# Hybrid attention and convolution block: the first two seven-product column pairs in turns, their operand sets spread over more products, and a spare weight buffer in the place of the convolution's tiles

## The chip, the cores and the metric

One core of one Trainium2 chip runs the whole kernel. The metric is the device time of one execution in microseconds (us); lower is better. A result is the median of several runs.

## The reference

One layer of a residual block over 2048 tokens of 1024 features, in float32:

```python
h    = rmsnorm(x, norm_g)
proj = einsum('bsd,de->bse', h, w_in)         # 1024 -> 6144 columns
q, k, v, z_att, gb, gc, u, z_conv, g_att, g_conv = split(proj)
att    = chunked_rel_attention(q, k, v, rel_bias)   # 8 heads, own chunk of 64 and 8 to the left
y_att  = (att * silu(z_att)) @ w_att_out
vconv  = causal_depthwise_conv(gc * u, conv_w, conv_b)   # width 3
y_conv = (gb * vconv * silu(z_conv)) @ w_conv_out
m   = sigmoid(g_att) * y_att + sigmoid(g_conv) * y_conv
out = rmsnorm(x + m @ w_out, final_norm_g)
```

Eight of the ten column groups of `w_in` have 512 columns, the two gates (`g_att`, `g_conv`) 1024 each.

## The kernel before

**Numbers.** Every matmul is made of three passes (`passes`, L132 to L137): each operand is split into a high part and a remainder, and high x high, high x low and low x high are added up. A split (`split_into` L122 and L123, `split_pair` L128 and L129, `raw_split` L344 and L345) is a cast on ScalarE and a subtraction on VectorE.

**Stages.** The projection runs over two halves of 1024 tokens, each over 24 pairs of column tiles (2 x 128 columns). A half of tokens is two blocks of 512 (c = 0, 1), the 1024 features are two halves (k = 0, 1), and a pair is two column tiles (n = 0, 1): a 2 x 2 x 2 block product. It is done with seven products in place of eight (`ORDER = (1, 2, 6, 5, 7, 4, 3)`), each 12 matmuls of 128 x 512. Its left operands are combinations of the pair's four weight blocks (`operand`, L375 to L399), its right operands combinations of the four token blocks b11, b12, b21, b22 (`operand_steps`, L348 to L363: product 1 uses b11, 2 uses b21, 6 uses b11 + b12, and so on). The seven results are put together by VectorE as they come (L749 to L769), and an evacuation function takes each finished 128 x 512 tile on: gates go through tanh and to memory from ScalarE's DMA queue (`ev_gate`), the convolution's pairs go through `conv_pair`, queries, keys and values to memory. The attention runs later, beside the second half's products; then come the output projections.

**The start.** The normalization needs sums over the tokens, which are not there at once. The first `PLAIN = 3` pairs of the first half are therefore done as plain products: 12 groups q = 0 to 11, in the order pair, token block c, column tile n, each of 24 matmuls on tokens that are scaled by `norm_g` alone (`raw_split`), and the result is multiplied by the token's factor when it is evacuated (`scaled`, L607, the operation whose output is named `c`). For q below 4 ScalarE copies the bank out first. Beside these groups VectorE normalizes the token blocks (L304) and makes right operands for the seven-product pairs (tiles t1.. to t7.., named by product and feature tile: t10l is the low part of product 1's first). `between(q)` lists what is made after which group: it calls for a set of right operands at each q above 5 until five are made, and the last two follow beside the first seven products. Weights of the plain pairs are split by `weights0` (tiles `w0`) at the end of groups 2, 3, 6 and 7.

**What orders the work.** The part with the plain groups stands in a manual schedule: PE, VectorE and ScalarE run its operations in the order of the program. Outside of it a scheduler orders each engine's queue, and it also moves later operations up between those of the manual part. Each engine, and each DMA queue (SP's for loads and stores, ScalarE's for gate tiles), then goes through its queue strictly in order, so that an instruction that waits holds up all behind it. PSUM has three banks for these products (`ps_d`). Raw weights have four buffers of 512 KB (`ww`: two per pair), split weights four (`wr`, tile `wc` or `w0`), token blocks four (`xs`). The split weights of product s + 2 are made while product s runs; each `wc` is also stored to memory for the second half (L399), and the store of s - 2 must have landed before the buffer takes s + 2.

**Names.** I number the seven-product work of the first half from product 0, the first after the plain groups; pairs are counted from 0 in the order in which they run. Pairs 0 to 2 are plain. Pair 3 is a gate; before the change pairs 4 and 5 are the first two of the convolution, and four gates follow one by one between the other convolution pairs up to pair 15; pairs 16 to 23 are queries, keys, values and z. The convolution's tiles come from a pool `cva` that is open from the start.

Of the kernel before, what the change touches and what calls it, by code (L numbers as in the profile page):

```python
# [8 lines left out]
F32 = mybir.dt.float32  # L9
# [8 lines left out]
P = 128  # L18
# [5 lines left out]
CH = 512  # L24
# [16 lines left out]
def block_kernel(ctx, tc, xb, xt, wp_in, wy, wo, bias, ng, fg, cw, cb, out):  # L41
# [225 lines left out]
    s_pool = fp("s", 2)  # L267
    conv_stack = ExitStack()
    cva = conv_stack.enter_context(tc.tile_pool(name="cva", bufs=2))

    blocks = {}
    ops = {}
# [97 lines left out]
    def load_raw(p, n):  # L370
        r = ww.tile([P, 2, 4, P], F32, tag="w", name="wraw")
        raws[p, n] = r
        nc.sync.dma_start(r, wp_in[p % NPAIR, n])
# [89 lines left out]
    def conv_pair(b):  # L463
# [5 lines left out]
        def conv(c, x, y):  # L469
            a = cva.tile([P, 2 + CH], F32, tag="a", name="cva")  # L470
            av[c] = a
# [36 lines left out]
    conv_gate = lambda *g: [x for b in range(4) for x in (C + 2 * b, C + 2 * b + 1, *g[b:b + 1])]  # L508
    order = [[*range(G, G + 4), *conv_gate(G + 4, G + 5, G + 6, G + 7), *range(Q, Q + 8)]]
    order.append([G + 3, G + 4, *range(G, G + PLAIN), *range(Q, Q + 8), *conv_gate(), G + 5, G + 6, G + 7])  # L510
# [49 lines left out]
    mid0, mid1 = names[PLAIN:NPAIR - 2], names[NPAIR + 2:]  # L560
    seq = [(p, i) for p in mid0 for i in ORDER]
    seq += together(*names[NPAIR - 2:NPAIR], ending)
# [18 lines left out]
    for sb, src in ((cw_sb, cw), (cb_sb, cb)):  # L581
        nc.sync.dma_start(sb, src)
    warm = ep.tile([P, CH], BF16, tag="e", name="warm")
    nc.vector.memset(warm, 0.0)
# [45 lines left out]
    def between(q):  # L630

        if q == 4 or q == 5:
            for k in range(8):
                normalize(tt_[q - 4][k], k, rb[q - 4])
        elif q == 6:
            for j in range(4):
                third(0, j)
        if q in (6, 7):
            for n in range(2):
                copied.pop(0)()  # L640
        if q > 5 and len(built) < 5:
            built.append(next(steps))
# [67 lines left out]
    for s, (p, i) in enumerate(seq):  # L710
        half = p // NPAIR
        n = names.index(p)
        if due and due[0] <= s:
            due.pop(0)
            next(turned)
        if half == 0 and i == 1 and n + 1 < NPAIR:
            for k in range(2):
# [5 lines left out]
        while nw < min(len(seq), s + ahead + 1):  # L723
            operand(*seq[nw])
            nw += 1
        if half == 0 and len(built) < 7 and s:
            built.append(next(steps))
# [58 lines left out]
        if n == NPAIR + 2 + PLAIN + 16 and i == 1:  # L786
            conv_stack.close()
            gp = pool("gp", 5)
# [178 lines left out]
```

## Time and profile before

| what | us |
|---|---|
| median of three runs | 1554.11 |
| lowest and highest of them | 1553.26, 1556.15 |
| the profiled execution, its own time | 1557.6 |
| its span, first to last instruction | 1555.8 |
| TensorE busy in the span | 1516.6 |
| VectorE, ScalarE busy | 1039.7, 680.1 |
| mean granted clock of TensorE | 0.992 |

Busy time of TensorE is the time in which any matmul is in flight; since matmuls overlap, a busy TensorE is not one at its peak, and the pace is read from the distance of their starts. The granted clock is the share of full speed that TensorE was given. A row of waits says who waited for whom, how long in total, how often, and the longest. In the rows in order of time the first number is the start in us from the start of the span, the second the duration, and the bracket gives the engine's idle time before the row and what ended it. `PEld` is the load of weights into TensorE, which overlaps the matmuls; `SPq` and `ACTq` are the queues that issue DMA.

### The profile page before, as it was taken

What the parts mean: (1) busy time and instruction counts of PE and PEld (TensorE: products, weight loads), DVE (VectorE), ACT (ScalarE), POOL (GpSimd) and SP (SyncE); (2) the same over time, 40 slices, a digit from 0 to 9 for tenths busy, and PEclk for the clock granted to TensorE, in tenths of its full rate; (3) what the DMA queues carried; (4) which work ended last, traced back from release to release, by engine and by line L of the source; (5) the groups of instructions that cost most, each with busy time, mean ns of one, the idle gap of its engine ahead of it and who ended that gap; (6) DMA issues with size and microseconds to landing.
All of it is one profiled execution on the core that took longest, in us unless ns stands there. A gap on an engine that the chain in (4) does not pass through costs nothing.

```text
span 1555.8 us, 21590 instructions
## 1 busy us (share of the span) xinstructions
PE 1516.6 (97%) x7396; PEld 1267.9 (81%) x7396; DVE 1039.7 (67%) x2078; ACT 680.1 (44%) x1250; POOL 155.0 (10%) x294
## 2 busy tenths in 40 slices
PE   9899999999998999999999999999999999999997
PEld 6678888888776788888888888888888888888886
DVE  7977789796668654666666767677755574445544
ACT  6353353443325343555666556666665231112111
POOL 0000000000000001223222222322220000000000
PEclk9999999999999999999999999999999999999999
DMA  5288999988987835999898776888889945365131
GB/s 209 77 285 307 339 353 327 364 310 305 319 301 262 279 122 177 329 339 341 294 290 272 228 265 228 262 261 272 263 278 322 304 162 200 102 233 193 62 109 68
DMA packets 159406, 389.45 MB, mean 250 GB/s; under 512 B 19904, under 2 KB 40384, under 8 KB 159296
## 3 DMA queue, kind: packets, MB, share of 16 engines
q1 hardware_dynamic: 129088, 302.06, 56.2%
q0 software_dynamic: 20992, 69.22, 13.6%
q10 hardware_dynamic: 9216, 16.78, 2.9%
q8 instruction: 59, 0.97, 0.3%
q14 instruction: 51, 0.42, 0.1%
HBM read 236.99 MB, written 150.99 MB: 249 GB/s over the span
## 4 chain that ended last, share of the span: by engine, by line
PE 83%; DVE 9%; ACT 2%; DMA 2%; issue 2%; POOL 0%; SPq 0%; ACTq 0%; DVEq 0%; POOLq 0%
PE ps_d L137 20%; PE ps_d L135 20%; PE ps_d L136 20%; PE ps_d L876 4%; PE ps_d L874 4%; PE ps_d L875 4%; PE ps_s L190 4%; PE po L228 4%; PE ps_t L210 3%; DVE ptl L216 1%; DVE ps_s L196 1%; DMA wc<-wc 1%; DVE xs L304 1%; ACT pr L200 1%; DMA vv<-v 0%
## 5 line engine op out<-in xcount | busy, mean ns | idle before, releaser
L200 ACT ACTIVATE pr<-ps_s,nmax 128x640 f32<-128x640 f32 (+4 forms) x128 | 93.4, 730 | 96.7 <-DVE nmax L196 96.1
L158 POOL DMA_DIRECT2D q<-q x128 | 66.7, 526 | 681.3 <-DVE wc L123 602.5
L196 DVE CUSTOM_DVE_ANT_0 ps_s<-ps_s,bs 128x640 f32<-128x640 f32 (+4 forms) x128 | 95.4, 745 | 53.8 <-PE ps_s L190 53.2
L122 ACT CAST wc<-wraw 128x512 fp32r<-128x512 f32 x120 | 73.6, 621 | 114.2 <-PE ps_d L137 94.2
L202 ACT ACTIVATE pr<-pr,rs 128x640 f32<-128x640 f32 (+4 forms) x128 | 97.8, 764 | 27.3 <-DVE rs L201 27.2
L190 PE MATMUL ps_s<-kk,q 128*128 128x320 f32 (+1 forms) x448 | 97.4, 333 | 2.9 <-ACT pr L200 2.8
L135 PE MATMUL ps_d<-mid,wy 128*128 128x512 f32 x256 | 99.6, 389 | 0.0
L136 PE MATMUL ps_d<-mid,wy 128*128 128x512 f32 x256 | 99.6, 389 | 0.0
L137 PE MATMUL ps_d<-mid,wy 128*128 128x512 f32 x256 | 99.6, 389 | 0.0
L216 DVE TENSOR_TENSOR ptl<-ps_t,pth 128x640 fp32r<-128x640 f32 (+4 forms) x128 | 94.3, 736 | 6.6 <-ACT pth L215 6.0
L215 ACT CAST pth<-ps_t 128x640 fp32r<-128x640 f32 (+4 forms) x128 | 80.0, 625 | 41.0 <-PE ps_t L210 40.0
L123 DVE TENSOR_TENSOR wc<-wraw,wc 128x512 fp32r<-128x512 f32 x120 | 82.2, 689 | 13.7 <-ACT wc L122 13.5
L210 PE MATMUL ps_t<-ident,pr 128*128 128x128 f32 x560 | 83.9, 276 | 1.1 <-DVE ptl L216 0.6
L883 ACT ACTIVATE sq<-y 128x512 f32<-128x512 f32 x32 | 20.2, 632 | 146.0 <-DVE y L878 141.3
L228 PE MATMUL po<-pth,vv 128*128 128x256 f32 x336 | 79.1, 271 | 1.8 <-DMA vv<-v 1.6
L228 PE MATMUL po<-ptl,vv 128*128 128x256 f32 x336 | 78.3, 281 | 0.2 <-DVE ptl L216 0.2
L874 PE MATMUL ps_d<-wo,mh 128*128 128x512 f32 x192 | 74.7, 389 | 0.0
L875 PE MATMUL ps_d<-wo,mh 128*128 128x512 f32 x192 | 74.7, 389 | 0.0
L876 PE MATMUL ps_d<-wo,ml 128*128 128x512 f32 x192 | 74.7, 389 | 0.0
L190 PEld LDWEIGHTS ps_s<-kk,q 128*128 128x128 f32 x448 | 67.0, 190 | 7.8 <-ACT pr L200 7.4
L878 DVE SCALAR_TENSOR_TENSOR y<-ps_d,y 128x512 f32<-128x512 f32 x32 | 22.1, 692 | 76.0 <-PE ps_d L876 75.9
L210 PEld LDWEIGHTS ps_t<-ident,pr 128*128 128x128 f32 x560 | 63.2, 140 | 11.4 <-DVE ptl L216 2.1
(370 smaller groups left out, 4183.8 us busy)
## 6 DMA issues: line engine op xcount, KB each, us to landing
wc<-wc SPq DMA_DIRECT2D x294, 512.0 KB, 4.8
wraw<-wp_in SPq DMA_DIRECT2D x54, 512.0 KB, 5.9
q<-q POOLq DMA_DIRECT2D x128, 128.0 KB, 4.9
gl<-gate SPq DMA_DIRECT2D x64, 256.0 KB, 3.2
mid<-mid SPq DMA_DIRECT2D x64, 256.0 KB, 5.2
bs<-bias POOLq DMA_DIRECT2D x32, 320.0 KB, 7.2
gate<-c ACTq DMA_DIRECT2D x34, 256.0 KB, 4.7
v<-vst SPq DMA_DIRECT2D x64, 128.0 KB, 4.7
```

The source lines that it names most:

```text
L135: nc.tensor.matmul(ps, lhsT=w[:, 0, k, :], rhs=rh[:, cs], start=(first and k == 0), stop=False)
L136: nc.tensor.matmul(ps, lhsT=w[:, 0, k, :], rhs=rl[:, cs], start=False, stop=False)
L137: nc.tensor.matmul(ps, lhsT=w[:, 1, k, :], rhs=rh[:, cs], start=False, stop=(last and k == len(rhs) - 1))
L190: nc.tensor.matmul(ps[:, i, :m], lhsT=q[s][:, g * P:(g + 1) * P], rhs=kk[:, k1 - n + i * m:k1 - n + (i + 1) * m], start=(s == 0), stop=(s ...
L196: nc.vector.tensor_tensor_reduce(out=view, in0=view, in1=bv, scale=-0.125, scalar=3.0e38, op0=ALU.add, op1=ALU.min, accum_out=nmax)
L200: nc.scalar.activation(out, view, AF.Exp, bias=nmax, scale=-1.0, accum_out=rs)
L210: nc.tensor.transpose(out=ps[:, j * P:(j + 1) * P], in_=pr[:, j * P:(j + 1) * P], identity=ident)
L216: nc.vector.tensor_sub(lo[:, js, qs], src, hi[:, js, qs].bitcast(F32))
L228: nc.tensor.matmul(ps[:, (g0 + a) * P:(g0 + b) * P], lhsT=vv[:, g0 + j, :], rhs=s[:, j, a * P:b * P], start=(i == 0 and s is pt[0]), stop= ...
L874: nc.tensor.matmul(ps, lhsT=mh[:, gs], rhs=wh, start=(k == 0), stop=False)
L875: nc.tensor.matmul(ps, lhsT=mh[:, gs], rhs=wl, start=False, stop=False)
L876: nc.tensor.matmul(ps, lhsT=ml[:, gs], rhs=wh, start=False, stop=(k == KT - 1))
```

## The change

Five things are edited.

- **Order of the pairs.** The first half's gates 4 and 5 now run as pairs 4 and 5, directly after pair 3, and the convolution starts with pair 6. Gates 6 and 7 stay between convolution pairs.
- **Pairs 3 and 4 in turns.** Their fourteen products run as 1, 2 of pair 3, then 1, 2 of pair 4, then 6 of both, 5 of both, 7 of both, 4 of both, 3 of both.
- **Right operands.** `between(q)` asks for one set after group 6 and one after group 7 (products 1 and 2). The other five are asked for at every odd product from product 1 on.
- **Loads.** Pair 4's raw weights are loaded in the row of early loads, and no longer at pair 3's first product. Pair 5's first half goes into a buffer of its own.
- **The spare buffer.** A pool `extra` (one buffer of 512 KB) takes the place at which the pool `cva` stood; at the first product of pair 6 it is closed and `cva` is opened there.

```diff
-    conv_stack = ExitStack()
-    cva = conv_stack.enter_context(tc.tile_pool(name="cva", bufs=2))
+    spare = ExitStack()
+    extra = spare.enter_context(tc.tile_pool(name="extra", bufs=1))
+    pools = []
...
     def load_raw(p, n):
-        r = ww.tile([P, 2, 4, P], F32, tag="w", name="wraw")
+        r = (extra if (p, n) == (names[PLAIN + 2], 0) else ww).tile([P, 2, 4, P], F32, tag="w", name="wraw")
...
-            a = cva.tile([P, 2 + CH], F32, tag="a", name="cva")
+            a = pools[0].tile([P, 2 + CH], F32, tag="a", name="cva")
...
-    order = [[*range(G, G + 4), *conv_gate(G + 4, G + 5, G + 6, G + 7), *range(Q, Q + 8)]]
+    order = [[*range(G, G + 6), *conv_gate(G + 6, G + 7), *range(Q, Q + 8)]]
...
-    seq = [(p, i) for p in mid0 for i in ORDER]
+    seq = together(*mid0[:2], [*((i, k) for k in range(2) for i in (1, 2)), *((i, k) for i in ORDER[2:] for k in range(2))])
+    seq += [(p, i) for p in mid0[2:] for i in ORDER]
...
+    for k in range(2):
+        load_raw(4, k)
...
-        if q > 5 and len(built) < 5:
+        if q in (6, 7):
             built.append(next(steps))
...
-        if half == 0 and i == 1 and n + 1 < NPAIR:
+        if n == PLAIN + 3 and i == 1:
+            spare.close()
+            pools[:] = [spare.enter_context(tc.tile_pool(name="cva", bufs=2))]
+        if half == 0 and i == 1 and PLAIN < n < NPAIR - 1:
             for k in range(2):
                 load_raw(names[n + 1], k)
...
-        if half == 0 and len(built) < 7 and s:
+        if half == 0 and len(built) < 7 and s % 2:
             built.append(next(steps))
...
         if n == NPAIR + 2 + PLAIN + 16 and i == 1:
-            conv_stack.close()
+            spare.close()
```

What the scheduler makes of it is seen in the queues. VectorE before the change, from the evacuation of group 5 (`c_980`) to a little behind that of group 6 (`c_1033`); `w0_984` and `w0_987` are the weights of pair 2's first column tile, used by groups 8 and 10, `w0_1041` and `w0_1044` those of its second, used by groups 9 and 11; `xs` are token blocks:

```order
L607 TENSOR_TENSOR c_980<-ps_p_891,rb_836 128x512
L123 TENSOR_TENSOR w0_984<-wraw_538,w0_984 128x512
L123 TENSOR_TENSOR w0_987<-wraw_538,w0_987 128x512
...
L129 TENSOR_TENSOR t23l_1030<-xs_523,t23h_1029 128x512
L607 TENSOR_TENSOR c_1033<-ps_p_933,rb_909 128x512
L123 TENSOR_TENSOR w0_1041<-wraw_540,w0_1041 128x512
L123 TENSOR_TENSOR w0_1044<-wraw_540,w0_1044 128x512
L354 TENSOR_TENSOR xs_517<-xs_517,xs_528 128x512
L356 TENSOR_TENSOR xs_523<-xs_523,xs_517 128x512
L129 TENSOR_TENSOR t60l_1074<-xs_517,t60h_1073 128x512
```

The second column tile's weights stand directly behind group 6's evacuation, ahead of product 6's operands. The same place after the change (`c_1037` is group 6, `c_1076` group 7, `c_1109` group 8, `w0_1045` and `w0_1048` the second column tile's weights):

```order
L612 TENSOR_TENSOR c_1037<-ps_p_937,rb_913 128x512
L358 TENSOR_TENSOR xs_523<-xs_523,xs_517 128x512 x2
L129 TENSOR_TENSOR t60l_1207<-xs_517,t60h_1206 128x512
L358 TENSOR_TENSOR xs_523<-xs_523,xs_517 128x512 x2
L129 TENSOR_TENSOR t61l_1212<-xs_517,t61h_1211 128x512
L123 TENSOR_TENSOR w0_1045<-wraw_540,w0_1045 128x512
L123 TENSOR_TENSOR w0_1048<-wraw_540,w0_1048 128x512
L612 TENSOR_TENSOR c_1076<-ps_p_994,rb_913 128x512
L612 TENSOR_TENSOR c_1109<-ps_p_1051,rb_840 128x512
L129 TENSOR_TENSOR t62l_1217<-xs_517,t62h_1216 128x512
L129 TENSOR_TENSOR t63l_1222<-xs_517,t63h_1221 128x512
L392 TENSOR_TENSOR s1_1274<-wraw_550 128x512
```

Six operations of product 6 now stand between group 6's evacuation and the second column tile's weights, although the program asks for product 6's set only later, and groups 7 and 8 are evacuated back to back; `s1_1274` reads pair 4's second weight half, the first VectorE instruction that does.

SP's queue after the change, where it comes to the next half's token blocks (`xs`, from `xb`); `wc4_3` is the store of pair 4's product 3, `wc5_1` and so on those of pair 5, `wraw` raw weights:

```order
L375 DMA wraw_1577<-wp_in 128x1024
L401 DMA wc4_3_318<-wc_1515 128x1024
L401 DMA wc5_1_324<-wc_1535 128x1024
L281 DMA xs_1590<-xb 128x1024
L281 DMA xs_1593<-xb 128x1024 x2
L281 DMA xs_1596<-xb 128x1024 x2
L401 DMA wc5_2_325<-wc_1555 128x1024
L401 DMA wc5_6_329<-wc_1579 128x1024
```

Five loads of token blocks stand together there, between the stores of pair 5's first two operands; before, four of the eight loads stood ahead of pair 3's first store, and the other four came by one and two between the stores of the next two pairs.

## The prediction

> **What bounds the kernel now.** I read the page first, then the waits of TensorE, then the busy time by stages of 20 us, then the order of time on TensorE and VectorE where the stages show idle time. The page's head: one core, and TensorE has 39 us of its span idle.
>
> ```profile
> span 1555.8 us, 21590 instructions
> PE 1516.6 (97%) x7396; PEld 1267.9 (81%) x7396; DVE 1039.7 (67%) x2078; ACT 680.1 (44%) x1250; POOL 155.0 (10%) x294
> ```
>
> Who TensorE waited for, over the whole span (total, times, longest):
>
> ```profile
> PE ps_p L135 <- DVE c L607: 9.1, 3, 3.6
> PE ps_d L137 <- DVE wc L123: 6.0, 4, 3.6
> ```
>
> The largest is the plain products' wait for VectorE to empty a bank. By stages (busy time of PE, PEld, DVE, ACT, POOL, then granted clock, DMA share and rate):
>
> ```profile
> 40.00:60.00 20.00, 17.62 (x80) 14.25 (x78) 19.96 (x34) 7.72 (x15) 0.00 (x0) 1.00 0.11 40
> 60.00:80.00 20.00, 16.85 (x66) 13.32 (x67) 17.84 (x30) 7.27 (x12) 0.00 (x0) 0.91 0.32 106
> 80.00:100.00 20.00, 16.39 (x60) 12.93 (x59) 12.91 (x21) 11.21 (x20) 0.00 (x0) 0.83 0.75 243
> 100.00:120.00 20.00, 20.00 (x90) 16.57 (x89) 16.84 (x28) 10.44 (x18) 0.00 (x0) 1.00 0.99 351
> ```
>
> From 40 to 60 us VectorE is full, TensorE loses 2 to 4 us per stage, and from 60 to 100 its clock drops too. At 100 all is dense. So what this change can be worth lies between 57 and 94 us. There, TensorE in order of time (start, duration, in brackets the idle time before it):
>
> ```profile
> 60.09 0.47 PE L135 MATMUL ps_p<-rawh,w 128*128 128x512 f32 x1 [2.46 <-DVE c L607]
> 76.00 0.50 PE L135 MATMUL ps_p<-rawh,w 128*128 128x512 f32 x1 [3.07 <-DVE c L607]
> 85.34 0.79 PE L135 MATMUL ps_p<-rawh,w 128*128 128x512 f32 x1 [3.61 <-DVE c L607]
> 93.80 0.39 PE L135 MATMUL ps_d<-t10h,wc 128*128 128x512 f32 x1
> 94.48 0.39 PE L135 MATMUL ps_d<-t11h,wc 128*128 128x512 f32 x1
> ```
>
> The three waits stand at the starts of plain groups 8, 10 and 11; 93.80 is mixed product 0. The last two rows give the pace: three matmuls in 0.68 us, 0.227 each, so a group of 24 takes 5.44 us and a product of 12 takes 2.72 us. VectorE's rows that release these groups:
>
> ```profile
> 59.25 0.69 DVE L607 TENSOR_TENSOR c<-ps_p,rb 128x512 f32<-128x512 f32 x1
> 59.85 1.29 DVE L123 TENSOR_TENSOR w<-wraw,w 128x512 fp32r<-128x512 f32 x2
> ...
> 64.65 0.70 DVE L607 TENSOR_TENSOR c<-ps_p,rb 128x512 f32<-128x512 f32 x1
> 65.25 1.30 DVE L123 TENSOR_TENSOR w<-wraw,w 128x512 fp32r<-128x512 f32 x2
> ...
> 75.25 0.69 DVE L607 TENSOR_TENSOR c<-ps_p,rb 128x512 f32<-128x512 f32 x1
> ...
> 77.89 0.69 DVE L129 TENSOR_TENSOR t50l<-t,t50h 128x512 fp32r<-128x512 f32 x1 [1.35 <-ACT t50h L128]
> ...
> 84.61 0.68 DVE L607 TENSOR_TENSOR c<-ps_p,rb 128x512 f32<-128x512 f32 x1
> ```
>
> I call the evacuation of group q c(q): these are c5, c6, c7, c8. Group q starts when c(q-3) is done: c5 ends at 59.94 and group 8 starts at 60.09, c7 ends at 75.94 and group 10 starts at 76.00, c8 ends at 85.29 and group 11 at 85.34. c5 begins at 59.25 and its successor at 59.85, so an operation of 512 columns costs 0.60 us of VectorE in a row (its 0.69 overlaps the next). Between c6 and c8 lie the operands of products 6 and 5, and the latter also wait for ScalarE.
>
> **The clock.** I asked for TensorE's busy time and granted clock in stretches of 3.41 us, laid so that one ends at 64.20:
>
> ```profile
> 57.37:60.79 3.42, 0.96 (x5) 0.99 0.38 143
> 60.79:64.20 3.41, 3.41 (x9) 0.51 0.72 225
> 71.03:74.44 3.41, 1.90 (x9) 1.00 0.00 0
> 74.44:77.85 3.41, 1.85 (x8) 1.00 0.47 176
> 81.27:84.68 3.41, 0.46 (x3) 0.99 0.09 16
> 84.68:88.09 3.41, 2.75 (x7) 0.50 0.86 265
> 88.09:91.51 3.42, 3.42 (x10) 0.51 1.07 262
> 91.51:94.92 3.41, 3.41 (x16) 1.00 0.80 262
> 412.36:415.77 3.41, 1.46 (x6) 0.99 0.91 356
> 415.77:419.19 3.42, 3.34 (x9) 0.51 0.81 319
> 419.19:422.60 3.41, 3.41 (x17) 1.00 0.74 221
> ```
>
> The same grid fits 8 and 104 stretches later. After a stretch with 1.95 us or more idle the next runs at half clock; 1.56 idle (74.44) does not do it; a half-clock stretch with 0.66 idle (84.68) is followed by another. A full slow stretch costs 1.7 us. Before mixed product 0 the two cost 3.0: 85.34 and 5.44 make 90.8, and it began at 93.80. [...]
>
> **The change, part by part.** *Operands moved out of the plain products.* Up to c5 VectorE has the same 13 operations after c4 (two additions of product 6 stand where two combinations of pair 3's weights stood), so group 8 starts at 60.09 as before. Then one addition comes ahead of weights(2,0): they end at 61.14, 0.6 later, and group 8's third matmul waits for them; it loses about 0.4. c6 now has 12 operations between it and c5 in place of 8: 59.25 + 13 x 0.60 = 67.05, done at 67.74, which is when group 8 ends. Next is the point that decides: weights(2,1) stood right behind c6, and now six operations of product 6 (four subtractions, two low parts) stand between. Their low part begins at 67.05 + 7 x 0.60 = 71.25 and ends at 71.94. Group 9 runs its first two matmuls at 67.8 and stands at the third until 72.0: a new stall of 3.7 us. Behind it c7 (72.45) and c8 (73.05) are done by 73.75, before groups 10 and 11 want them. So both old stalls, 3.07 and 3.61, go, and this one comes. From 72.0 stand 22 matmuls of group 9 and 48 of groups 10 and 11: 70 x 0.227 = 15.9, and mixed product 0 starts at 87.9 without clock loss, against 90.8: 2.9 earlier.
>
> *Pair 4's weights among the early loads.* The second half can only load when weights(2,1) has been read, at 72.5; VectorE reads it right after product 6's last low part (74.95).
>
> ```profile
> wraw<-wp_in SPq DMA_DIRECT2D x2, 512.0 KB, 4.0
> ```
>
> 4.0 us (this row: 60 to 80 us) put it at 76.6: VectorE stands 1.7 us, with c9 queued behind, and product 0 waits for c9. Group 9 ends at 77.0 or later, so c9 could not be earlier than 77.0, and product 0 needs it at 87.9. Nothing, unless the landing takes 14 us.
>
> *Products of pairs 3 and 4 in turns.* Each operand set serves two products, 5.44 us. Walking VectorE's queue with 0.60 us per operation from product 0 at 87.9 (ScalarE has less to do: 10.44 against 16.84 us in the stage from 100), product 6 (104.2) needs the low part of its weights, done at 101.5, and its last operand, at 102.1, two us after it starts: a margin of 2.7. Products 8, 10 and 12 have 2 or more. Weights for product s+2 need the store of s-2 to have landed; of that below. Cost: nothing; the cover is VectorE's lead, and if it were gone, one product would slip by what is missing.
>
> *Gate pairs 4 and 5 ahead of the convolution.* VectorE's work per pair, counted by the order, peaks at 19.3 + 18.8 us in pairs 15 and 16 against 19.05 of TensorE per pair; before, 18.7 + 18.5 in 14 and 15, without a wait. A lag of 1 to 2 us fits in the three banks (5.4 us). Nothing. From pair 17 on, and all of the second half, the three queues stand as before, so the rest shifts as a whole.
>
> *Spare buffer.* Pair 5's first weights load at about 20 us into idle queues; the convolution's tiles come there two pairs after its last reader. Nothing: all that moves beside it is one copy of two columns.
>
> **The clock term** decides the size. I take the phase as free and move the grid through its 3.41 us. Before: group 9 ends at 71.0 to 72.7, and the idle time up to 76.0 mostly fills a stretch well enough to slow group 10. That is free: with 1.7 to 3.0 us lost group 10 ends at 83.1 to 84.4, still ahead of c8 (85.29), and what idle time is left is too short to slow group 11. This holds in 59 of 100 phases, product 0 at 90.8; in 20 one slow stretch falls on group 11, 92.5; in 21 a boundary halves the idle time as 74.44 did here, group 10 runs fast, ends at 81.4 and leaves 3.6 idle: 93.8. Mean 91.8. After: nothing behind the new stall waits for VectorE, so every slow stretch counts. A boundary between 68.3 and 69.95 (49 of 100 phases) leaves 2 us or more idle in the stretch that follows it, and the next is slow: 1.8. One between 69.95 and 70.35 (12) halves the stall: none. One between 70.35 and 71.7 (39) makes it slow before the restart, and the unfull stretch keeps it slow for another: 2.9. Mean 2.0: product 0 at 89.9. So 91.8 - 89.9 = 1.9 us of gain on the mean, 3.9 against the profiled execution (1557.6, of it 1.8 around the span), which had the costly phase: it would come to 1553.7. The three timed runs have their median at 1554.1, 3.5 below the profiled one; a lucky phase here and at the later waits, 1.7 a piece, would explain that. Forecast: 1554.1 - 1.9 = 1552.2.
>
> **Rivals.** *The clock costs both alike.* If the phase is tied to the program's start, or the clock falls only after a wholly idle stretch, no clock term is left: -2.9, 1551.2. For it: one profile can't show the phase of another run. Against it: the row of 412.36, and 2.9 us between the fastest and the slowest of three runs. [...]
>
> *Before pays the clock and after does not*: 93.8 against 87.9, -5.9, 1548.2. It needs the profile's phase to be the rule and 12 of 100 phases on the other side.
>
> *The moved loads of x crowd the stores (slower).* Five loads of 512 KB now stand on SP between the stores of pair 5's first two operands, issued at 120 to 127 us. Times to landing now, 95 to 130 us, and how full the DMA is:
>
> ```profile
> wc<-wc SPq DMA_DIRECT2D x14, 512.0 KB, 5.9
> ...
> xs<-xb SPq DMA_DIRECT2D x4, 512.0 KB, 6.9
> ```
>
> ```profile
> 123.00:128.00 5.00, 5.00 (x23) 4.13 (x22) 2.71 (x5) 1.25 (x2) 0.00 (x0) 1.00 1.02 393
> ```
>
> At 393 GB/s, from 107 to 127 us I count 9.7 MB to move where 7.9 fit: 1.8 MB or 4.7 us of backlog. The store behind the five loads, issued at 127, then lands near 135.5; its buffer is wanted by 138.2 (product 19 at 139.6, less a cast and a subtraction). Each us beyond 138.2 is one of TensorE's, and from 2 on a slow stretch is added. A landing 6 us later than I reckon gives 3.3 + 1.7 = 5.0 lost, +3.1; at 7 us it is +4, 1558. Against it: before, 40 us of full DMA passed without a wait.
>
> *The stalls only change places*: another wait of 2 us in pairs 3 to 5 that I missed, for instance on product 6's weights; no gain, 1554.
>
> **How the numbers follow.** 0.2% is 3.1 us, about what a measurement of this kernel can tell from no change. Forecast 0.56, clock alike 0.16, before pays alone 0.10, crowding 0.07, only changed places 0.11. Faster by over 0.2%: 0.10 from the forecast's phases, 0.06 of the first rival, 0.09 of the second: 0.25. Slower by over 0.2%: 0.06. Same: 0.69. The range goes from 1549.0 (between the two faster rivals) to 1555.5 (a phase that costs after 3.0 and before nothing is +0.3, and a slip of one us).
>
> **What the changed profile would show.** Right: a wait of about 3.7 us at the third matmul of group 9 for the low part of a weight, near 68 to 72 us; no wait at the starts of groups 10 and 11; c7 and c8 back to back; mixed product 0 between 87.9 and 91.1; dense from there to 400. Wrong: a wait of ScalarE or VectorE for a store near 135 us followed by TensorE; product 0 later than 91.5; or a low part of weights(2,1) well before 71.

## The result and the profile after

The changed kernel takes 1563.77 us (median of 5 runs, 1559.25 to 1566.4); the kernel before took 1553.26 us beside it (5 runs, 1550.5 to 1556.15). The ratio is 1.0063, 95% interval 1.0044 to 1.0082: some 10 us slower, where the forecast was 1552.2 and the range ended at 1555.5.

The head of the page and the waits of TensorE's plain products in the changed kernel (total, times, longest):

```profile
span 1561.6 us, 21575 instructions
PE 1515.1 (97%) x7396; PEld 1264.1 (81%) x7396; DVE 1038.0 (66%) x2078; ACT 679.4 (44%) x1250; POOL 155.0 (10%) x294
...
PE ps_p L137 <- DVE w L123: 3.7, 2, 3.4
PE ps_p L135 <- DVE c L612: 2.9, 2, 2.5
```

The plain products' wait for an evacuation has gone from 9.1 to 2.9 us, and a wait for a weight's low part has come (3.7). So the start did what was forecast, but for 0.48 us in front of the new stall. TensorE in order of time there, and mixed product 0:

```profile
60.13 0.76 PE L135 MATMUL ps_p<-rawh,w 128*128 128x512 f32 x1 [2.46 <-DVE c L612]
67.96 0.47 PE L135 MATMUL ps_p<-rawh,w 128*128 128x512 f32 x1 [0.48 <-DVE c L612]
72.08 0.80 PE L137 MATMUL ps_p<-rawh,w 128*128 128x512 f32 x1 [3.42 <-DVE w L123]
90.33 0.39 PE L135 MATMUL ps_d<-t10h,wc 128*128 128x512 f32 x1
```

Mixed product 0 starts at 90.33, 3.47 us earlier than in the profile before. This lead is still there at 200 us. Then it is lost. The stages of the changed kernel (busy PE, PEld, DVE, ACT, POOL, granted clock, DMA share, GB/s):

```profile
120.00:140.00 20.00, 20.00 (x90) 16.55 (x89) 12.75 (x21) 7.38 (x12) 0.00 (x0) 1.00 1.03 401
180.00:200.00 20.00, 20.00 (x90) 16.58 (x89) 14.85 (x26) 9.54 (x20) 0.00 (x0) 1.00 0.86 295
200.00:220.00 20.00, 16.44 (x69) 12.35 (x68) 12.61 (x33) 8.61 (x19) 0.00 (x0) 1.00 1.01 379
220.00:240.00 20.00, 19.97 (x83) 16.35 (x84) 17.97 (x34) 8.88 (x17) 0.00 (x0) 0.91 0.94 343
380.00:400.00 20.00, 17.97 (x78) 14.28 (x77) 13.69 (x22) 6.19 (x11) 0.00 (x0) 1.00 0.91 315
```

TensorE is full up to 200 us. In the stage from 200 it has 16.44 of 20, while VectorE (12.61) and ScalarE (8.61) aren't full either and the DMA is: no engine has too much to do, so some engine waits for a transfer. The gaps of TensorE between 90 and 410 us:

```profile
202.27 0.47 PE L135 MATMUL ps_d<-t30h,wc 128*128 128x512 f32 x1 [0.26 <-DVE v L764]
215.16 0.50 PE L137 MATMUL ps_d<-t50h,wc 128*128 128x512 f32 x1 [0.93 <-DVE wc L123]
220.03 0.56 PE L135 MATMUL ps_d<-t70h,wc 128*128 128x512 f32 x1 [2.31 <-DVE c L757]
398.92 0.50 PE L135 MATMUL ps_d<-t40h,wc 128*128 128x512 f32 x1 [1.95 <-ACT wc L122]
403.67 0.50 PE L137 MATMUL ps_d<-t30h,wc 128*128 128x512 f32 x1 [0.93 <-DVE wc L123]
```

Against the kernel before the starts of the products slip by 6.31 us between pairs 8 and 14 (from 3.47 earlier to 2.84 later; 20 x 0.09 = 1.8 us of it is the clock of 0.91 behind the gap at 220), and by 3.87 us more in pair 18. The kernel before has none of these gaps. Of the 3.87 us, 1.5 come back in pair 19: there both kernels have a gap of 1.95 us, but the kernel before loses 4.1 us in that pair, with the slow stretch at 415.77 that the prediction shows, and the changed kernel 2.6, at full clock. VectorE ahead of the gaps at 202 and 220 us in the changed kernel, and the place of the second in the kernel before:

```profile
200.59 0.33 DVE L523 TENSOR_SCALAR bias<-bias 128x320 f32<-128x320 f32 x1 [3.93 <-DMA bias<-bias]
...
213.50 0.33 DVE L523 TENSOR_SCALAR bias<-bias 128x320 f32<-128x320 f32 x1 [1.59 <-DMA bias<-bias]
...
217.87 0.69 DVE L392 TENSOR_TENSOR s<-wraw 128x512 f32<-128x512 f32 x1 [1.75 <-DMA wraw<-wp_in]
218.60 0.69 DVE L393 TENSOR_TENSOR s<-s,wraw 128x512 f32<-128x512 f32 x1
219.21 0.68 DVE L757 TENSOR_TENSOR c<-u,ps_d 128x512 f32<-128x512 f32 x1
```

```profile
212.76 0.32 DVE L521 TENSOR_SCALAR bias<-bias 128x320 f32<-128x320 f32 x1
...
213.07 0.69 DVE L390 TENSOR_TENSOR s<-wraw 128x512 f32<-128x512 f32 x1
...
213.79 0.69 DVE L391 TENSOR_TENSOR s<-s,wraw 128x512 f32<-128x512 f32 x1
...
215.55 0.68 DVE L749 TENSOR_TENSOR c<-u,ps_d 128x512 f32<-128x512 f32 x1
```

Both queues hold the same thing: the sums of the *next* pair's weights (L392, L393; L390, L391 before) stand ahead of the *present* pair's first evacuation by VectorE (L757; L749), though they are needed only by the next pair. Before, their raw weights have landed and it costs nothing. Now VectorE stands 1.75 us for them, behind it the evacuation, behind that TensorE. The small gap at 202 comes in the same way behind the scaling of a bias, for whose read VectorE stands 3.93 us. SP issued the read of these raw weights at 209.87, and in the kernel before at 202.27; in the changed kernel SP itself stood 2.2 us ahead of it, by the profile until a gate tile's store had landed:

```profile
209.87 1.69 SPq L375 DMA_DIRECT2D wraw<-wp_in  x2
```

```profile
202.27 1.70 SPq L373 DMA_DIRECT2D wraw<-wp_in  x2
```

Pair 10 would have begun at 223.6 without the loss, and begins at 227.07 before: the read has 13.7 us instead of 24.8. Two pieces of work that the change does not touch move through these pairs: `norm_steps(1)`, the norm of the second token half, which reads its tokens in tiles of 256 KB (`xt`) in three steps per pair from pair 8 on, and `reduce_bias`, which reads, scales and stores one half head's bias twice per pair from pair 6 on. They are placed by the number of the pair, so they stayed where they were while the convolution moved two pairs later.

### The profile page after: what moved, and what is told of

Same layout as the page of the kernel before. It is cut to its first block, busy times and chain, and to the rows that moved or that the text cites. A ratio compares the mean times of both kernels' runs of the same rounds, so it can differ in the third digit from the quotient of the medians.

```text
span 1561.6 us, 21575 instructions
## 1 busy us (share of the span) xinstructions
PE 1515.1 (97%) x7396; PEld 1264.1 (81%) x7396; DVE 1038.0 (66%) x2078; ACT 679.4 (44%) x1250; POOL 155.0 (10%) x294
## 4 chain that ended last, share of the span: by engine, by line
PE 76%; DVE 10%; DMA 7%; issue 3%; ACT 2%; POOL 1%; SPq 0%; DVEq 0%; ACTq 0%; POOLq 0%
PE ps_d L137 18%; PE ps_d L135 18%; PE ps_d L136 17%; PE ps_d L883 4%; PE ps_d L884 4%; PE ps_d L882 4%; PE po L228 3%; PE ps_s L190 3%; PE ps_t L210 3%; DMA wc<-wc 2%; DMA vv<-v 1%; DVE ptl L216 1%; DMA wraw<-wp_in 1%; DMA gate<-c 1%; DVE ps_s L196 1%
```

## Experiments

Times are compared by the ratio to runs of the kernel before on the same chip (medians there 1552.9 to 1554.8). "Lost at 9-10" is what the starts of the products slip in a kernel's profile against those of before from pair 7 to pair 14, with the clock that comes of it (where the norm starts at pair 6: pairs 6 to 9), "pair 18" what that pair takes over 19.04 us.

| kernel | median us | ratio, 95% interval | lost at 9-10 | pair 18 |
|---|---|---|---|---|
| changed | 1563.77 | 1.0063 (1.0044 to 1.0082) | 6.3 | 3.9 |
| order_only | 1562.53 | 1.0068 (1.0051 to 1.0085) | 2.3 | 3.8 |
| x1_later | 1552.92 | 0.9998 (0.9985 to 1.0012) | 0 | 1.8 |
| bias_later | 1556.95 | 1.0039 (1.0019 to 1.0058) | 2.2 | 3.9 |
| both_later | 1557.96 | 1.0041 (1.0025 to 1.0057) | 0 | 4.2 |
| before_x1_early | 1555.20 | 1.0011 (0.9993 to 1.0029) | 2.1 | 0 |
| gates_after | 1559.20 | 1.0029 (1.0016 to 1.0042) | 2.1 | 3.9 |
| gate_last | 1552.98 | 0.9992 (0.9978 to 1.0006) | 0 | 1.2 |
| g7_back | 1557.85 | 1.0026 (1.0011 to 1.0041) | 5.2 | 0 |
| bias_slack | 1559.79 | 1.0035 (1.0020 to 1.0049) | 2.1 | 3.9 |
| raw_early | 1556.53 | 1.0019 (1.0003 to 1.0035) | 2.0 | 3.1 |
| raw_early_slack | 1556.96 | 1.0017 (1.0001 to 1.0034) | 1.1 | 3.1 |
| sums_pool | 1570.82 | 1.0102 (1.0078 to 1.0126) | 15.2 | 5.3 |
| sums_pool_all | 1563.62 | 1.0067 (1.0043 to 1.0091) | 8.0 | 5.1 |
| set_later | 1547.34 | 0.9959 (0.9942 to 0.9976) | 0 | 1.8 |
| set_gate | 1546.83 | 0.9960 (0.9943 to 0.9977) | 0 | 1.3 |
| set_latest | 1542.09 | 0.9927 (0.9909 to 0.9945) | 0 | 1.8 |
| all_mends | 1540.85 | 0.9927 (0.9901 to 0.9953) | 1.2 | 0 |

### Which part of the change loses the time

The kernel before with one line of the change:

```
-    order = [[*range(G, G + 4), *conv_gate(G + 4, G + 5, G + 6, G + 7), *range(Q, Q + 8)]]
+    order = [[*range(G, G + 6), *conv_gate(G + 6, G + 7), *range(Q, Q + 8)]]
```

> The kernel before with the new order of the pairs alone: gates of pairs 4 and 5 ahead of the convolution, everything else as it was (no turns, five right operand sets as before, no spare buffer). Theory A: the meeting of the x1 reads with the stores comes with the order, so this loses about 6 us against the kernel before, 1559 to 1562 us, ratio 1.004 to 1.006, with gaps near 205 to 225 us. Theory D (the early part of the change, its turns and its early weight reads, leaves a lag that comes out at 200 us): no loss, ratio 0.999 to 1.001.

It loses as much as the whole change, 1.0068. Its gaps:

```profile
133.18 0.47 PE L135 MATMUL ps_d<-t20h,wc 128*128 128x512 f32 x1 [1.12 <-DVE u L765]
...
219.77 0.47 PE L135 MATMUL ps_d<-t70h,wc 128*128 128x512 f32 x1 [2.03 <-DVE c L749]
...
397.06 0.50 PE L135 MATMUL ps_d<-t40h,wc 128*128 128x512 f32 x1 [1.95 <-ACT wc L122]
401.82 0.50 PE L137 MATMUL ps_d<-t30h,wc 128*128 128x512 f32 x1 [0.93 <-DVE wc L123]
```

So the order of the pairs is enough for the whole loss, with gaps at the same two places (220 us and pair 18) and without turns, spare buffer and moved operand sets; theory D falls. The gap at 133 us is this kernel's own. The slips (1.37 at 133, 2.32 at 220, 3.84 in pair 18) add up to 7.5 us, the medians say 10.6: its profiled execution was its fastest (1559.34), and that of before (1557.6) is above its median. The 3 us between are not assigned: at the start of pair 20 this profile is 4.6 us behind that of before, at the end of the span 1.7, so what lies behind pair 19 differs by 3 us between two executions.

### The norm, the bias and the stores meet in pairs 8 and 9

```
-        if half == 0 and 8 <= n < 22 and i in (2, 5, 4):
+        if half == 0 and 10 <= n < 22 and i in (2, 5, 4):
             next(x1, None)
```

> The changed kernel with one number different: the norm of the second token half starts at pair 10 and not at pair 8 (34 steps in 36 places). In the changed kernel's profile eight of its token reads (256 KB each) fall into pair 8, into the same 19 us as the four stores of the first convolution pair and the first gate stores behind it; the bias scaling waits 3.93 us for its read there and stands at the head of VectorE's row, and 6.3 us are lost from 202 to 240 us. Theory A (this meeting of reads and stores loses the time): the 6.3 us go, 1557 to 1558 us, 1.0025 of the kernel before, and the gaps at 202, 215 and 220 us are not in its profile. Theory B (the bias reads alone are too early for their place): no change, 1562 to 1565 us. Theory C (gates next to the convolution load VectorE and ScalarE, whatever moves beside them): no change, and the gaps stand at the same products.

The ratio is 0.9998 in place of 1.0063: one number gives back some 10 us, more than theory A asked. Beside the 6.3 us, pair 18 loses 1.8 us and not 3.9. Theories B and C fall. No gap is left between 90 and 390 us:

```profile
200.00:220.00 20.00, 20.00 (x90) 16.57 (x89) 13.49 (x24) 6.12 (x10) 0.00 (x0) 1.00 1.00 370
```

The DMA's share is hardly lower (1.00 for 1.01), and TensorE is full. VectorE waits 0.8 us for bias from 180 to 240 us where it waited 5.7, and the read of pair 10's weights is issued at 198.03, 24.6 us before pair 10:

```profile
198.03 1.68 SPq L375 DMA_DIRECT2D wraw<-wp_in  x2
```

The edit moves the norm's reads and the norm's operations on VectorE together and doesn't tell them apart. The bias instead of the norm, and both (`6 <= n < 22` to `8 <= n < 24`):

> The changed kernel with the bias scaling of the 32 half heads at pairs 8 to 23 and not 6 to 21; the norm of the second half stays at pair 8. Theory A (eight token reads meet the convolution's stores in pair 8): the bias reads stay in pairs 8 and 9, the loss stays, 1562 to 1566 us. Theory B (the bias reads): only those of pairs 6 and 7 go, so that a wait moves but stays; no change or some us less, 1558 to 1564. Theory C: no change.

> The changed kernel with both moved by the two pairs by which the convolution moved: norm of the second half from pair 10, bias scaling from pair 8. The convolution, the gates behind it, the token reads and the bias reads then stand to each other as in the kernel before. Theory A: as with the norm alone, 1556 to 1558 us; what is left over 1553 would be the gaps at 398 and 404 us, which come from somewhere else. Theory C: 1562 to 1565 us.

Moving the bias gives back 4 of the 6.3 us at 9-10 (some 1.8 of the 6.3 are the clock of 0.91 from 220 us on in the changed kernel), though its reads then begin in pair 8. That is against theory A as I had put it: the bias is a party to the meeting, and not only a victim. With both moved nothing is lost there, as theory A has it, but pair 18 loses 4.2. The bias now runs on to pair 23; that this is why was not tested.

The meeting without the new order:

> The kernel before, its order of pairs untouched, with the norm of the second token half started at pair 6 and not at pair 8, so that the eight token reads of the first pair fall on the stores of the first convolution pair (pair 5) and on the gate stores of pair 6, as they do in the changed kernel two pairs later. Theory A (the meeting loses the time): 1557 to 1561 us, ratio 1.003 to 1.005, with new gaps between 160 and 185 us. Theory C (the gates' new place itself): no change, ratio 0.999 to 1.001.

A miss for theory A: 1.0011, and the interval holds 1. The profile has the new gap where it was expected (1.35 us at 180.81 for an evacuation, and VectorE waiting 4.1 us for raw weights and 3.7 for bias), 2.1 us with what follows. In the old order the reads of the norm and the stores of the convolution are thus not enough for 6 us. The gate moved behind the convolution's second pair:

```
-    order = [[*range(G, G + 6), *conv_gate(G + 6, G + 7), *range(Q, Q + 8)]]
+    order = [[*range(G, G + 6), *range(C, C + 4), G + 6, C + 4, C + 5, G + 7, C + 6, C + 7, *range(Q, Q + 8)]]
```

> The changed kernel with the second convolution pair pulled ahead of the gate: pairs 6 to 9 are the convolution's, pair 10 the gate, then convolution, convolution, gate. Norm of the second half from pair 8 as in the changed kernel. The four stores of the first convolution pair still meet the eight token reads in pair 8, but no gate stores follow them in pairs 8 and 9. Theory A as it stands (reads and the convolution's stores are enough): the loss of some 6 us at pairs 9 and 10 stays, 1562 to 1565 us. Theory A with the gate stores as a needed part: the loss goes, 1555 to 1559 us.

1559.2 us, between the two theories: 2.1 us are lost. But the edit does more than take the gate's stores away, since the convolution's second pair comes in the gate's place and brings VectorE its work. Ahead of the gap that is left (1.52 us, again before L757) VectorE waits for nothing:

```profile
215.22 0.68 DVE L392 TENSOR_TENSOR s<-wraw 128x512 f32<-128x512 f32 x1
...
216.55 0.68 DVE L757 TENSOR_TENSOR c<-u,ps_d 128x512 f32<-128x512 f32 x1
```

From 207 us on its row is full without a wait, with the convolution's operations, a dozen small ones of the norm (0.15 to 0.17 us each) and the sums ahead of the evacuation. So this run doesn't give the share of the gate's stores. What is shown: move the norm away and the loss goes; move the bias alone and a third of it stays. That the number of transfers in these two pairs decides is a reading and not shown: from 195 to 222 us the DMA moves 366 GB/s in the changed kernel, 366 with the bias moved and 367 here.

### How the late transfers reach TensorE

> The changed kernel with one number different: the scaling of a half head's bias follows its read by six products and not by three (16.3 us and not 8.2 us), so that VectorE doesn't stand waiting for the read (5.7 us in three waits between 185 and 225 us, the longest 3.93 us). Theory G (the late transfers reach TensorE by way of VectorE's row: the bias scaling at its head holds back the weights' low parts and the evictions): the loss of 6.3 us at pairs 9 and 10 goes, 1557 to 1559 us. Theory H (they reach it by the weights' own stores and reads, which are late by themselves): VectorE's waits for bias go, the loss stays, 1561 to 1565 us.

The edit is `defer(3, go)` to `defer(6, go)`. Neither theory comes out clean. The loss falls from 6.3 to 2.1 us and the time to 1559.79, but VectorE still waits 5.2 us for bias, in three waits as before: the queue changed under the edit, and the waits moved to places where TensorE didn't wait for what stood behind them. A gap of 1.82 us stays before L757, behind 2.0 us of waiting for the raw weights. Theory H's wait exists too. From 180 to 240 us ScalarE's casts of weights wait for stores to land, in the changed kernel and in the one before:

```profile
ACT wc L122 <- DMA wc<-wc: 11.2, 8, 4.2
```

```profile
ACT wc L122 <- DMA wc<-wc: 6.8, 3, 4.0
```

With the norm at pair 10 there is no such wait, but with the bias slack it grows to 15.5 us while the loss falls to a third, so by itself it doesn't set the loss. The raw weights, one product earlier:

```
-        if half == 0 and i == 1 and PLAIN < n < NPAIR - 1:
+        if half == 0 and ((i == 1 and n == PLAIN + 1) or (i == 3 and PLAIN < n < NPAIR - 2)):
             for k in range(2):
-                load_raw(names[n + 1], k)
+                load_raw(names[n + (1 if i == 1 else 2)], k)
```

> The changed kernel with the raw weights of the next pair read one product earlier: in SP's row they move ahead of one bias read and one weight store. In the changed kernel the two reads of pair 10's weights are issued at 209.9 us, 13.7 us before pair 10 would begin (24.8 us before in the kernel before), and VectorE waits 1.75 us for them ahead of the eviction that TensorE waits 2.31 us for. Theory I (two ways: bias scaling and raw weights, both at the head of VectorE's row): the wait for the raw weights shrinks, 1.5 to 3 us are gained, 1560 to 1562 us. Rival (the raw weights are late by the traffic and not by their place): no change, 1562 to 1565 us.

> The same with the bias scaling six products behind its read as well. Theory I: no gap of over 0.5 us between 195 and 240 us with the norm still at pair 8 and the same bytes moved; with only the loss of pair 18 (3.87 us) left, 1556 to 1558 us. Rival (the traffic itself is too much for that stretch): a gap of 1 to 2 us stays before the first eviction of pair 9 or moves to pair 10, 1558 to 1560 us.

The read is issued at 201.8 us in place of 209.9, and the loss falls to 2.0 us, with the bias slack to 1.1 (again some 1.8 us of what is won are the clock). Theory I gains, in more than its size; but the gap before the first evacuation doesn't go: 1.79 and 0.84 us. In the first kernel VectorE's wait for the raw weights doesn't shrink but grows from 1.75 to 2.91 us: it now comes to the first sum 6.7 us earlier, ahead of the bias scaling and not behind it. So the place in VectorE's row counts as much as the time of the issue. In the second kernel VectorE waits 0.8 us for the raw weights and 7.0 us for bias. Last, the sums themselves on GpSimd, without and with the difference of product 7 that stands beside them:

```
+            eng = nc.gpsimd if 8 <= names.index(p) < 14 else nc.vector
-            nc.vector.tensor_add(s1, a21, a22)
-            nc.vector.tensor_sub(src, s1, a11)
-            nc.vector.tensor_sub(a12, a12, src)
+            eng.tensor_add(s1, a21, a22)
+            eng.tensor_sub(src, s1, a11)
+            eng.tensor_sub(a12, a12, src)
```

> The changed kernel with the three weight sums of product 6 done by GpSimd and not by VectorE in pairs 8 to 13; reads, stores and their order stay. In the changed kernel VectorE waits 1.75 us for the raw weights of pair 10 at the first of these sums, which stands ahead of the first eviction of pair 9, and TensorE waits 2.31 us for that eviction at 220 us. Theory I: that gap goes; what is left at pairs 9 and 10 is what the bias scaling holds back (gaps of 0.26 and 0.93 us), 1559 to 1561 us. Rival (the late transfers hold TensorE by more than this place): a gap of 1.5 us or more stays between 200 and 240 us, on VectorE or on a cast, 1562 to 1565 us, or later if GpSimd's own time for the sums is long.

> As the run before, with the difference for product 7 on GpSimd as well: no sum of the next pair's weights is left on VectorE in pairs 8 to 13. Theory I: the gap before the first eviction of pair 9 goes, and what is lost at pairs 9 and 10 falls from 6.3 us to 1 to 3 us (the bias scaling's share), 1558 to 1562 us. Rival: 4 us or more stay lost there, 1562 us or more.

The first is a miss that tells something. The difference left on VectorE waits for GpSimd in the same place, and TensorE's gap grows from 2.31 to 4.54 us; pairs 7 and 8 lose 4.3 us already. The waits of VectorE there and the gap:

```profile
DVE wraw L399 <- POOL s L393: 7.9, 2, 4.7
...
225.51 0.77 PE L135 MATMUL ps_d<-t70h,wc 128*128 128x512 f32 x1 [4.54 <-DVE c L758]
```

In the second the evacuation follows the operation before it without a wait (VectorE in order of time), and the gap at 220 us is gone:

```profile
212.03 0.68 DVE L758 TENSOR_TENSOR c<-u,ps_d 128x512 f32<-128x512 f32 x1
```

Up to 235 us it has lost some 1.5 us where the changed kernel has lost 6.3; by 280 us it has lost 8.0. But at 227.5, 236.9 and 257.0 come gaps of 1.19, 0.97 and 2.52 us, and its median is as high as that of the changed kernel. The last is for a bank that ScalarE empties, and ScalarE waits for VectorE, which is slow beside GpSimd's sums:

```profile
253.59 1.71 POOL L399 TENSOR_TENSOR wraw<-wraw 128x512 f32<-128x512 f32 x1
254.09 1.75 DVE L496 TENSOR_TENSOR cv<-cv,v 128x512 f32<-128x512 f32 x1
255.88 0.62 ACT L413 CAST hi<-cv 128x512 fp32r<-128x512 f32 x1 [3.94 <-DVE cv L496]
256.41 0.58 ACT L754 COPY u<-ps_d 128x512 f32<-128x512 f32 x1
```

So the place on VectorE is the way by which the late read reached pair 9: worse with a longer wait there, gone without it. The time is not won by this edit, since GpSimd's sums cost VectorE time in their turn (more on that in the last section), and the lag comes out two pairs later. What the place alone is worth these two runs therefore can't say.

### Pair 18

> The kernel with the norm at pair 10, with the last gate moved from pair 11 back to pair 15, between the convolution and the Q pairs, where the kernel before has it. In the profiles of all kernels with the new order, pair 18 is 1.83 to 4.2 us longer than 19.04 us (gaps of 1.5 to 1.95 us in it); the kernel before has no gap there. Theory E (Q pairs straight behind the convolution start with VectorE, ScalarE and the queue behind): pair 18 takes 19.04 us, 1.8 us or more are gained, 1549 to 1551.5 us, ratio 0.998 to 0.999: faster than the kernel before. Rival: the gap at pair 18 stays or moves, 1552 to 1554 us.

> The changed kernel with the last gate moved from pair 11 back to pair 15, behind the convolution, where the kernel before has it; norm at pair 8 and bias at pair 6 as in the changed kernel. Moving that gate together with the later norm left 1.22 us of gap in pair 18 instead of 1.83. Theory E (what is lost in pair 18, 3.87 us in the changed kernel, comes from the convolution ending straight ahead of the Q pairs): pair 18 takes 19.0 to 19.1 us as in the kernel before, 1559 to 1560 us. Rival (it comes from where the norm's and the bias's last steps stand to it): pair 18 still loses 1.2 us or more.

The last gate goes from pair 11 back to pair 15, between the convolution and the Q pairs, with the norm at pair 10 in the first and at pair 8 in the second:

```
+    order = [[*range(G, G + 6), C, C + 1, G + 6, *range(C + 2, C + 8), G + 7, *range(Q, Q + 8)]]
```

With the norm at 8, pair 18 takes 19.04 us and has no gap, as theory E says: the 3.87 us of the second loss come from ending the convolution straight ahead of the Q pairs. With the norm at 10, 1.22 us stay, which theory E doesn't explain, and `gate_last` gains nothing measurable over `x1_later`; so where the norm's last steps fall counts too. What sets the 1.22 is open.

### The new stall at the start

```
-        if q in (6, 7):
+        if q in (7, 8):
             built.append(next(steps))
```

> The kernel with the norm at pair 10, and the two operand sets beside the plain products at groups 7 and 8 and not at 6 and 7. The stall of 3.42 us at group 9's third matmul (all kernels with the new start have it, at 72 us) comes in the forecast from the six operations of product 6's operand that stand ahead of the weights of that group on VectorE. Theory F (as forecast): that stall goes; if nothing takes its place mixed product 0 starts up to 3.4 us earlier, at 86 to 88 us against 89.3 us, 1549.5 to 1552 us. Rival: the moved sets come late at the next group or at mixed product 0, and the 3.4 us are spent there, 1552 to 1554 us.

> The fastest kernel so far (norm at pair 10, operand sets beside groups 7 and 8), with the last gate at pair 15 as well. In the profiles the gate's move took 0.6 us off pair 18: 1546 to 1548 us, no difference that can be measured against 1547.3, ratio 0.995 to 0.996 to the kernel before.

> The fastest kernel so far with the two operand sets one group later again, beside groups 8 and 9. In its profile group 8's third matmul still waits 2.21 us for the weights' low part, with eight operations of operands and sums ahead of it on VectorE. Theory F: with the set moved behind those weights the 2.21 us go, and mixed product 0 starts at 84 us and not at 86.0 us, 1545 to 1546 us. Rival: the second set is then too late for the third and fourth mixed product, and as much is lost there: 1547 to 1549 us.

On top of the norm at pair 10, one group later gains 0.9998 - 0.9959 = 0.39% or 6 us, and groups 8 and 9 (`q in (8, 9)`) another 0.32% or 5. The stall of 3.42 us at group 9 goes to 2.21 (at group 9 too, and not at group 8 as the last expectation has it) and then away: between group 6's evacuation and the weights stand six VectorE operations, then four, then one. Mixed product 0 starts at 83.53 us in `set_later`, 5.8 earlier than in `x1_later` (the expectation's 86.0 is not in its profile). The stall of 2.46 us at 60 us, which the forecast took as given, goes with the first step, since the set of product 1 had stood ahead of group 5's evacuation on VectorE and now stands behind it. In the fastest of these kernels TensorE has no gap from 35 to 379 us (stages as above; then the start of mixed product 0):

```profile
40.00:60.00 20.00, 20.00 (x92) 16.54 (x91) 19.96 (x34) 6.68 (x12) 0.00 (x0) 1.00 0.22 58
60.00:80.00 20.00, 20.00 (x90) 16.57 (x89) 20.00 (x34) 11.58 (x21) 0.00 (x0) 1.00 0.53 188
...
79.15 0.39 PE L135 MATMUL ps_d<-t10h,wc 128*128 128x512 f32 x1
```

79.15 where the changed kernel has 90.33. The last gate adds nothing that can be measured (0.9960 for 0.9959).

> The changed kernel with the norm at pair 8 as it is and every other mend: raw weights one product earlier, bias scaling six products behind its read, the last gate at pair 15, operand sets beside groups 8 and 9. Against the fastest so far (1542.1 us, ratio 0.9927), which moved the norm instead and lost 1.82 us in pair 18. Theories E and I together: no gap in pairs 3 to 18, 1539 to 1541.5 us, ratio 0.991 to 0.9925. Rival: the start, 10 us earlier, brings new gaps at pairs 8 to 10, 1542 to 1545 us.

All mends with the norm left at pair 8 come to the same ratio, 0.9927: 1.2 us lost at pairs 9 and 10 (a gap of 0.87 us before L757 stays, against the expectation) for 1.8 us saved in pair 18. `set_latest`, the simpler of the two, beats both kernels: 11 us less than before.

## Why the prediction was wrong

**The start was right, to half a us per event.** VectorE in the changed kernel:

```profile
67.12 0.69 DVE L612 TENSOR_TENSOR c<-ps_p,rb 128x512 f32<-128x512 f32 x1
...
71.33 1.29 DVE L123 TENSOR_TENSOR w<-wraw,w 128x512 fp32r<-128x512 f32 x2
```

Evacuation c6 ends at 67.12 + 0.69 = 67.81 (forecast 67.74), the first low part of weights(2,1) at 71.33 + 0.69 = 72.02 (71.94), the new stall is 3.42 us (3.7) with 0.48 in front of it, and the two old stalls go. The VectorE operations ahead of the weights were the cause: with six the stall is 3.42 us, with four (`set_later`) 2.21, with one (`set_latest`) it is gone. Pair 4's weights cost nothing, though VectorE waits for them; the turns cost nothing, TensorE is full from 90.33 to 202. Twelve kernels with this start begin mixed product 0 between 89.24 and 90.33 us, 89.8 on the mean; three with the old one at 91.09, 92.26 and 93.80, 92.4. Forecast were 89.9 and 91.8, a gain of 1.9; it is 2.6, with only three profiles of the old start.

**The step that failed** is "Gate pairs 4 and 5 ahead of the convolution ... Nothing." Alone this order costs a ratio of 1.0068, 10.6 us, where the sum has nothing. I had counted what VectorE has to do per pair, 19.3 and 18.8 of 19.05 us, and asked whether that fits. It does: in the stage that loses, VectorE is busy 12.61 of 20 us. I had not counted what moves against what: the convolution and its stores went two pairs back, the norm and the bias, placed by pair number, did not, and from pair 8 on they met. Moving the norm by the same two pairs brings the ratio to 0.9998, which shows that the norm's place against the convolution makes the loss; which of the parts of that meeting weighs how much stays open (the norm's reads, its operations on VectorE, the bias, the gate's stores). Nor had I asked what in VectorE's queue waits for a transfer: the bias scaling and the next pair's weight sums, both ahead of evacuations.

**"From pair 17 on the three queues stand as before, so the rest shifts as a whole"** fails too. The rows of VectorE, ScalarE and SP are alike only from the end of pair 18 on (404 us before, 409 after), and there too for VectorE and ScalarE but for a few neighbours that change places. Behind the same operation of pair 18 stands, before and after:

```profile
387.38 0.69 DVE L411 TENSOR_TENSOR c<-c,hi 128x512 fp32r<-128x512 f32 x1 [0.69 <-ACT hi L410]
387.99 0.68 DVE L390 TENSOR_TENSOR s<-wraw 128x512 f32<-128x512 f32 x1
```

```profile
390.27 0.69 DVE L413 TENSOR_TENSOR c<-c,hi 128x512 fp32r<-128x512 f32 x1 [0.69 <-ACT hi L412]
390.88 0.68 DVE L123 TENSOR_TENSOR wc<-wraw,wc 128x512 fp32r<-128x512 f32 x1
```

The 3.87 us of pair 18 lie in that stretch, and `g7_back` shows that the gate's place makes them while the norm stands at pair 8.

**The rivals.** Crowding was named, with a chance of 0.07, for the token blocks at 120 to 140 us. There the DMA is at 1.03 and 401 GB/s, and TensorE stays full: that rival did not happen. Late transfers decided 80 us later, by way of VectorE's row, with reads that I had not looked at because the diff doesn't touch them. A full DMA is no sign by itself: TensorE stays full beside it at 120 us (a share of 1.03), and at 200 us in `x1_later` (1.00). What counts is whether an operation that TensorE needs soon stands behind the one that waits for the late transfer.

**The clock terms** can't be judged from the median, since the start's 2.6 us are lost under the rest; `order_only` and the changed kernel differ by less than their intervals. The starts of mixed product 0 bear the term for the new start out: 89.8 us on the mean where 87.9 was the sum without clock loss and 89.9 the one with it. No run shows that the phase is free and each phase as likely, on which the means 91.8 and 89.9 rest. What the profiles show in its place is mixed product 0 at 89.24 to 90.33 us with the new start and at 91.09, 92.26 and 93.80 with the old, and the gap of 1.95 us in pair 19 followed by a clock of 0.51 in the kernel before (from 415.77 us) and of 1.00 in the changed one (from 421.82).

## What to carry to other kernels

When work is reordered by pairs, stages or tiles, list also what is *not* moved but placed by the same numbers, and write down for each stretch which transfers now fall together. Then look in each engine's queue for the operations that wait for a transfer and ask what stands behind them: an operation that is needed much later can stand ahead of one that is needed now, and costs nothing until its data is late (here no gap of TensorE before the change, and one of 2.31 us after it). A count of busy time per stage, which is what I had, cannot see either.

## What the runs showed of the hardware

**The same stall costs differently by the clock.** The changed kernel and `x1_later` both stand 3.42 us at group 9; the granted clock (third number from the end) in stretches of 3.4 us behind it:

```profile
71.00:74.40 3.40, 2.32 (x6) 1.84 (x7) 3.40 (x7) 0.74 (x2) 0.00 (x0) 0.50 0.25 51
74.40:77.80 3.40, 3.40 (x11) 2.69 (x10) 2.01 (x4) 0.52 (x1) 0.00 (x0) 0.63 0.67 258
```

```profile
71.00:74.40 3.40, 2.45 (x6) 1.97 (x7) 3.40 (x7) 0.86 (x2) 0.00 (x0) 0.58 0.27 71
74.40:77.80 3.40, 3.40 (x16) 2.80 (x15) 1.88 (x3) 0.39 (x1) 0.00 (x0) 0.92 0.61 237
```

One is slow far into the second stretch, the other for little of it (0.63 and 0.92 over it; in the changed kernel the clock is 0.54 in the us from 76 and 1.00 in the us from 77). From the stall's end at 72.08 and 71.95, with 15.9 us for the 70 matmuls, mixed product 0 is 2.4 and 1.5 us late: it starts at 90.33 and 89.32. What sets how long the clock stays low after such a stall is not shown.

**VectorE is slow beside GpSimd's sums.** GpSimd's longest of the sums of two 128x512 tiles in `sums_pool` (busy, mean ns):

```profile
L394 POOL TENSOR_TENSOR s<-s,wraw 128x512 f32<-128x512 f32 x6 | 10.2, 1704 | 2.5 <-issue 2.1
```

That is 2.5 times VectorE's 0.68 to 0.69 us; the other two lines of sums have 1456 and 1481 ns, a factor of 2.1 to 2.2. In `sums_pool_all`, from 196 to 226 us, VectorE's operations on 128x512 tiles of SBUF take 0.69 us clear of GpSimd's sums, and 0.85, 0.97 and 1.36 us beside them; the one at 254.09 us above takes 1.75. In the changed kernel, without sums on GpSimd, the lines of the last two (L474 and L495 there) take 0.68 to 0.69 us. VectorE's evacuations out of PSUM take 0.68 to 0.69 us in both cases.
